# An encoder block on one core: the Fourier half scaled by ACT, its residual added later by an accumulating DMA, its wave tables made in two parts beforehand

## The chip, the core and the metric

The kernel runs on one NeuronCore of a Trainium2 chip. The core has engines that run side by side, each through its own instructions in order: TensorE (PE in the profile, with its weight loads as PEld), VectorE (DVE), ScalarE (ACT), GpSimd (POOL) and SyncE (SP), which here only issues DMAs. PE reads SBUF and writes PSUM. [...] POOL in this kernel works on SBUF alone and issues DMAs too. The metric is the time of the whole program on the device in microseconds, as the median of some runs. Before the change it is 2309.82 us (three runs, 2309.82 to 2311.7).

## What is computed

One layer of an encoder over 2048 tokens and 16 meta tokens (2064 in all), with 1024 channels, in float32. The input is normalized and projected once; a part of the projection goes to attention (4 query heads, 2 key and value heads of 128), a part, 4 groups of 128 channels, to a Fourier mix. Both halves are normalized by themselves, joined and projected back, and a residual is added; then comes an MLP of width 4096 with a squared relu, and a last normalization.

```python
f = jnp.fft.fft2(ug, axes=(1, 3), norm='ortho').real.astype(u.dtype)
y = jnp.einsum('blgc,gcd->blgd', f, w_f)
...
mixed = jnp.concatenate([rms_norm(attn, g_attn_out[i]), rms_norm(four, g_fourier_out[i])], axis=-1)
h = h + mixed @ w_out[i]
m = rms_norm(h, g_mlp[i])
h = h + jnp.square(jax.nn.relu(m @ w_up[i])) @ w_down[i]
...
return rms_norm(h, g_final)[:, N_META:]
```

The normalization of a half is one factor per token, so it can be applied after the product with `w_out`.

## The kernel before

**Products in parts.** A float32 operand of a large product is split in a high part (rounded by an ACT copy to `float32r`) and a low part (what is left, subtracted by DVE). `mm3` (L75 to L80) makes a product of three matmuls: high by high, high by low, low by high. The class `Split` makes the parts (L68 and L69; L71 and L72 with a factor). PE is thus fed by pairs of an ACT and a DVE instruction on nearly every operand.

**The stages in order.** First the input is normalized, transposed and projected (`prep`, `proj_u`, `proj_qkv`, `post`). The Fourier group's sequence is folded into even and odd parts in two large buffers, EV and UA. Then four transforms follow (`transform(0)` to `transform(3)`: cosine and sine, even and odd frequencies). Each makes partial sums `pa` over the channels, splits them into `ahi` and `alo`, and multiplies them with wave tables in `product`: 8 products `py` of 258 columns per transform, each summing over 2 (transforms 0 and 1) or 4 (2 and 3) full tables and one remainder table of 96 rows, which carries the high and low parts of a few rows in its own rows. `fourier` adds and subtracts the results back into EV and UA.

**Wave tables.** `load_tables` (from L484) loads a raw table of 128 rows and 516 columns by SP (L497), makes its high part by ACT (L503) and its low part by DVE (L506; L509 for 32 rows of the remainder table). There are 12 full and 4 remainder tables. Raw tables have 3 buffers, high parts 6, low parts 5. ACT's and DVE's table work of a transform is queued behind the last partial sums of the transform before (`last_acts`, `issue_after`).

**The Fourier half of the output projection.** `out_f` (L848 to L883) walks over 16 tiles of 128 tokens. For each it loads the tile of x into `xt` by SP (L859), splits the Fourier rows into `yh` and `yl`, and squares them by ACT (L869). POOL adds the four groups' squares in two steps, 256 and 128 columns wide (L872). PE sums them over the channels (L873), DVE and POOL make the factor `rf` from the sum (`rstd_of`, L188 and L190). Two halves of 512 columns are multiplied with `w_out` (`pof`), and DVE scales each by `rf` and adds x in one instruction (L881). The tile goes to `h_d` in DRAM by SP (L883).

**Attention beside it.** Attention runs in 16 units of 256 queries by 2 heads. Its scores, maxima, exponentials, sums and outputs `o` are interleaved with the transforms and with `out_f` by hand (`mix`, `att.upto`), and later with the MLP. The loads of queries, keys and values (q, kt, vt) are issued by POOL. Queries have one buffer, so a unit's queries are loaded when the scores of the unit before are done.

**The attention half.** `out_a(b)` (L937 on), for each of four blocks of 512 tokens, loads four tiles `h` from `h_d` by SP (L944), multiplies attention's output with `w_out` (`poa`), and DVE scales it by `ra` and adds it to `h` (L983). Then the MLP of the block follows (`transposes`, `up`, `down`, `final`).

**Order.** The program's text gives priorities; a planner assigns each engine's order, and that of the DMA queues, from its own estimates of when an operand is ready. So a load can stand earlier in a queue than in the text, but each queue is then run in that order: an instruction that waits holds up all that is behind it on its engine, DMA issues too.

Of the kernel before, what the change touches and what calls it, by code (L numbers as in the profile page):

```python
# [11 lines left out]
F32 = mybir.dt.float32  # L12
R32 = mybir.dt.float32r
AF = mybir.ActivationFunctionType
ALU = mybir.AluOpType
# [4 lines left out]
P = 128  # L20
# [14 lines left out]
REM = 96  # L35
MR = 96
CH = QUART // 2
CHP = 272
# [6 lines left out]
AHEAD = 30  # L45
FLEAD = 30
SKIP = 5
T_BUFS = (5, 6)
F_BUFS = (6, 7)
S_BUFS = 8  # L50
A_BUFS = 11
# [3 lines left out]
def f32v(ap):  # L55
    return ap.bitcast(F32)
# [26 lines left out]
def ins_of(x):  # L83
    return getattr(x, "ins", x)
# [49 lines left out]
def encoder_block(ctx: ExitStack, tc: tile.TileContext, x, meta, w_in, w_f,  # L134
                  w_out, w_up, w_down, g_fin, g_cols, g_rows, c_id, c_rope, c_dft, c_even, c_odd, c_rem, out):
    nc = tc.nc
    split = Split(nc)
    x = x[0]
    out = out[0]
# [58 lines left out]
    h_d = [dram.tile([P, D], F32, name=f"h_d{t}") for t in range(NT)]  # L198
# [273 lines left out]
        nc.vector.tensor_tensor(high, low, high, op=ALU.subtract)  # L472
        nc.scalar.copy(low, t)

    TW = 2 * CH
    last_acts = []
    ROWS = _rows()
    tables = {}

# [4 lines left out]
    def load_tables(tr):  # L484

        src, full, rest, n_tab = sources(tr)
        rem = ft.tile([P, NG, REM], F32, name=f"rem{tr}", tag="rem", bufs=1)
        nc.vector.memset(rem, 0.0)
        for o in (0, 32, 64):
            for lo, hi in rest:  # L490
                nc.vector.tensor_copy(rem[:, :, o:o + hi - lo], src[:, :, lo:hi])
                o += hi - lo
        tabs = []
        for nt in list(range(n_tab)) + [len(full)]:
            rows = P if nt < n_tab else REM
            raw = ft.tile([P, TW], F32, name=f"traw{tr}_{nt}", tag="traw", bufs=3)
            nc.sync.dma_start(raw[:rows], (c_even[tr, nt] if tr < 2 else c_odd[tr - 2, nt]) if rows == P else c_rem[tr])  # L497
            raw = raw.rearrange("p (c n) -> p c n", c=2)
            hi = ft.tile([P, 2, CHP], R32, name=f"thi{tr}_{nt}", tag="thi", bufs=T_BUFS[1])[:, :, :CH]
            with ExitStack() as behind:  # L500
                for i in last_acts:
                    behind.enter_context(tc.issue_after(i))
                nc.scalar.copy(hi[:rows], raw[:rows])  # L503
                if rows == P:
                    lo = ft.tile([P, 2, CHP], R32, name=f"tlo{tr}_{nt}", tag="tlo", bufs=T_BUFS[0])[:, :, :CH]
                    nc.vector.tensor_tensor(lo, raw, f32v(hi), op=ALU.subtract)  # L506
                    tabs.append((hi, lo))
                else:
                    nc.vector.tensor_tensor(hi[32:64], raw[32:64], f32v(hi[32:64]), op=ALU.subtract)  # L509
                    tabs.append(hi)  # L510
        tables[tr] = tabs, rem

    def transform(tr):

        src, full, rest, n_tab = sources(tr)
        if tr not in tables:
            load_tables(tr)
        tabs, rem = tables[tr]
        acts = []
        for nt in range(len(full) + 1):  # L520
            rows = P if nt < len(full) else REM
            ps = bank(f"pa{tr}_{nt}", (P, NG, P))
            for g in range(NG):
                a = src[:, g, full[nt]:full[nt] + P] if rows == P else rem[:, g, :]
                nc.tensor.matmul(ps[:rows, g, :], a, cw[tr % 2][:, g, :],
                                 start=True, stop=True)
            hi = fp.tile([P, NG, P], R32, name=f"ahi{tr}_{nt}", tag="ahi", bufs=F_BUFS[1])
            cp = nc.scalar.copy(hi[:rows], ps[:rows])
            if rows == P:
                lo = fp.tile([P, NG, P], R32, name=f"alo{tr}_{nt}", tag="alo", bufs=F_BUFS[0])  # L530
                nc.vector.tensor_tensor(lo, ps, f32v(hi), op=ALU.subtract)
                acts.append((hi, lo))
            else:
                sb = nc.vector.tensor_tensor(hi[64:96], ps[64:96], f32v(hi[64:96]), op=ALU.subtract)
                acts.append(hi)
                last_acts[:] = [ins_of(cp), ins_of(sb)]

        def product(g, c):
            ps = bank(f"py{tr}_{g}_{c}", (P, CH))
            for q in range(n_tab):  # L540
                hi, lo = acts[q + c * n_tab if tr < 2 else q]
                mm3(nc, ps, (hi[:, g, :], lo[:, g, :]), (tabs[q][0][:, c], tabs[q][1][:, c]), q == 0, False)
            nc.tensor.matmul(ps, acts[-1][:REM, g, :], tabs[-1][:REM, c], start=False, stop=True)
            return ps

        return product

    for j in range(LAST + 1):
# [16 lines left out]
        else:  # L565
            if j == 1:
                chan_dft()
            if j == LAST:
# [9 lines left out]
                ft = Lines(tc.alloc_tile_pool(name="ft", bufs=1, reuse_waits="tile"), small)  # L578
# [269 lines left out]
    def out_f():  # L848
        wt = {}
        for k in range(NG):  # L850
            for h in range(2):
                raw = wp.tile([P, 512], F32, name=f"wfr{k}_{h}", tag="wr", bufs=3)
                nc.sync.dma_start(raw, w_out[512 + k * P:512 + (k + 1) * P, h * 512:(h + 1) * 512])
                wt[k, h] = tuple(op_.tile([P, 512], R32, name=f"wf{e}{k}_{h}") for e in "hl")
                split(*wt[k, h], raw, c_fo(k))
            yield
        for t in range(NT):
            xt = op_.tile([P, D], F32, name=f"xo_{t}", tag="xo", bufs=2)
            nc.sync.dma_start(xt, x[t * P:(t + 1) * P, :])  # L859
            hi = op_.tile([P, NG, P], R32, name=f"yh_{t}", tag="yh", bufs=2)  # L860
            lo = op_.tile([P, NG, P], R32, name=f"yl_{t}", tag="yl", bufs=2)
            sq = op_.tile([P, NG, P], F32, name=f"ysq_{t}", tag="ysq", bufs=2)
            for par in range(2):
                for src, col, e, n in y_runs(par, 64 * t, 64 * t + 64):
                    y = src[:, :, col:col + n]
                    o = 2 * (e - 64 * t) + par
                    v = slice(o, o + 2 * n - 1, 2)
                    split(hi[:, :, v], lo[:, :, v], y)
                    nc.scalar.square(sq[:, :, v], y)  # L869
            ps = misc(f"pys_{t}", (P, 1))  # L870
            for n in (2, 1):
                nc.gpsimd.tensor_tensor(sq[:, :n], sq[:, :n], sq[:, n:2 * n], op=ALU.add)  # L872
            nc.tensor.matmul(ps, sq[:, 0], ones, start=True, stop=True)  # L873
            rf = rstd_of(op_, ps, 1, 512, "f")
            for h in range(2):
                ps = bank(f"pof_{t}_{h}")
                with tc.issue_after(ended[0]) if 2 * t + h >= 2 * NT - HELD else nullcontext():
                    for k in range(NG):
                        mm3(nc, ps, (hi[:, k, :], lo[:, k, :]), wt[k, h], k == 0, k == NG - 1)
                hs = slice(h * 512, (h + 1) * 512)  # L880
                nc.vector.scalar_tensor_tensor(xt[:, hs], ps, rf, xt[:, hs], op0=ALU.mult, op1=ALU.add)  # L881
                yield
            nc.sync.dma_start(h_d[t], xt)  # L883

# [52 lines left out]
    def out_a(b):  # L937

        b0, n = BLOCKS[b]
        T = 2 * n  # L940
        H[b] = hs = []
        for t in range(T):
            h = hps[b == 1].tile([P, D], F32, name=f"h_{b}_{t}", tag="h", bufs=4)
            nc.sync.dma_start(h, h_d[2 * b0 + t])  # L944
            hs.append(h)
        ps = misc(f"pas_{b}", (P, T))
        for t in range(T):
# [12 lines left out]
        for half in range(2):  # L960
            c = slice(half * 512, (half + 1) * 512)
# [29 lines left out]
        for t in range(T):  # L991
            nc.vector.scalar_tensor_tensor(part[t], sums[t][:, 1:2], 1.0 / D, part[t], op0=ALU.mult, op1=ALU.add)
            tag = "rs_m2" if b == 2 else "rs_m"
# [584 lines left out]
def _tables():  # L1578
# [13 lines left out]
    for tr in range(4):  # L1592
        starts, rest = _rows()[tr]
        token = _token(tr)
        if tr < 2:
            n_q = len(starts) // 2
            freq = [4 * np.arange(CH) + 2 + 2 * c for c in range(2)]
            full.append(np.stack([np.concatenate([_wave(tr, token(starts[c * n_q + q] + np.arange(P)), freq[c])
                                                  for c in range(2)], axis=1) for q in range(n_q)]))
        else:  # L1600
            freq = [2 * np.arange(c * CH, (c + 1) * CH) + 1 for c in range(2)]
            full.append(np.stack([_wave(tr, token(s0 + np.arange(P)), np.concatenate(freq)) for s0 in starts]))
        r = np.zeros((REM, 2 * CH), np.float32)
        for o in (0, 32, 64):
            for i, (lo, hi) in enumerate(rest):
                for c in ((i,) if tr < 2 else range(2)):
                    r[o:o + hi - lo, c * CH:(c + 1) * CH] = _wave(tr, token(np.arange(lo, hi)), freq[c])
                o += hi - lo
        rem.append(r)
    return np.eye(P, dtype=np.float32), rope, dft, np.stack(full[:2]), np.stack(full[2:]), np.stack(rem)  # L1610


_INS = ['x', 'meta_tokens', 'w_in', 'w_fourier', 'w_out', 'w_up', 'w_down', 'g_final']
# [27 lines left out]
```

## Time and profile before

| | |
|---|---|
| median of the runs | 2309.82 us |
| the profiled execution | 2310.59 us, of it 2308.8 us the span |
| PE busy | 2278.1 us (99% of the span) |
| weight loads busy | 1879.0 us (81%) |
| DVE busy | 1714.1 us (74%) |
| ACT busy | 1292.8 us (56%) |
| POOL busy | 204.6 us (9%) |
| moved by DMA | 307.23 MB |

The span runs from the first to the last instruction; the profiled execution's own time is a little longer. A row of a group of instructions has the line, engine and operation, out<-in by the program's names, the shapes and the count; after the bar the total busy time in us and the mean of one in ns; after the second bar the idle time of the engine just before them and what ended it. A row on one tile has the shortest, median and longest duration in ns and the first and last start in us. A row of waits reads: engine and line, what it waited for, the total in us, how often, the longest. PE's matmuls overlap, so that a busy PE can still lose time between two of them. DMA issues on POOL count as its instructions.

### The profile page before, as it was taken

Reading aid. Unit: us, or ns where it says so; the run is one execution under the profiler, and the core shown is the slowest. Engines: PE = TensorE matmul, PEld = TensorE weight load, DVE = VectorE, ACT = ScalarE, POOL = GpSimd, SP = SyncE. Lnnn points to the kernel's source line nnn. Section 1 sums busy time; section 2 is a strip of 40 time slices with the busy share of each in tenths; the row PEclk is TensorE's granted clock in tenths of the full one; section 3 lists DMA queues with packets and bytes.
Section 4 is the critical chain, followed back from the end, with each engine's and each line's share of the span. In section 5 each row is a group of like instructions: output and inputs, shape, how many; then the busy total and the mean of one; then the engine's idle time right before and its main releaser. Section 6 shows DMA issues by size and latency. Waiting matters only on the chain.

```text
span 2308.8 us, 29997 instructions
## 1 busy us (share of the span) xinstructions
PE 2278.1 (99%) x10822; PEld 1879.0 (81%) x10822; DVE 1714.1 (74%) x2431; ACT 1292.8 (56%) x2331; POOL 204.6 (9%) x244
## 2 busy tenths in 40 slices
PE   8999999999999999999999999999999999999998
PEld 7888987777788888888878888888888888888886
DVE  5435578999887876976886977886675656696786
ACT  6443355656675665665775675664555545543333
POOL 2212120233100000000000100000100000200000
PEclk9999999999999999999999999999999999999999
DMA  6343252543533322333242453325344444865442
GB/s 209 101 119 105 75 154 74 180 151 111 185 107 105 97 86 79 113 113 111 92 169 68 155 181 101 101 79 191 119 162 171 155 146 155 302 200 163 130 127 83
DMA packets 178069, 307.23 MB, mean 133 GB/s; under 512 B 14960, under 2 KB 63728, under 8 KB 177536
## 3 DMA queue, kind: packets, MB, share of 16 engines
q1 hardware_dynamic: 159280, 263.16, 34.7%
q0 software_dynamic: 18640, 42.16, 6.2%
q8 instruction: 85, 1.39, 0.2%
q14 instruction: 64, 0.52, 0.1%
HBM read 225.27 MB, written 79.99 MB: 132 GB/s over the span
## 4 chain that ended last, share of the span: by engine, by line
PE 70%; DVE 2%; DMA 1%; ACT 1%; issue 1%; POOL 0%; DVEq 0%; POOLq 0%; SPq 0%; ACTq 0%
PE pdn L78 5%; PE pdn L80 5%; PE pdn L79 5%; PE pup L80 5%; PE pup L78 5%; PE pup L79 5%; PE ux L78 2%; PE ux L79 2%; PE ux L80 2%; PE dx L78 2%; PE dx L79 2%; PE dx L80 2%; PE o L78 2%; PE o L79 2%; PE o L80 2%; PE s L78 2%
## 5 line engine op out<-in xcount | busy, mean ns | idle before, releaser
L78 PE MATMUL pup<-mT,wh_up 128*128 128x512 f32 x512 | 200.8, 393 | 0.7 <-ACT mT L71 0.7
L80 PE MATMUL pup<-mT,wl_up 128*128 128x512 f32 x512 | 200.9, 393 | 0.3 <-DVE wl_up L69 0.3
L79 PE MATMUL pup<-mT,wh_up 128*128 128x512 f32 x512 | 200.7, 392 | 0.0
L79 PE MATMUL pdn<-wl_dn,ah 128*128 128x512 f32 x512 | 200.6, 392 | 0.0
L78 PE MATMUL pdn<-wh_dn,ah 128*128 128x512 f32 x512 | 200.5, 393 | 0.0
L80 PE MATMUL pdn<-wh_dn,al 128*128 128x512 f32 x512 | 199.2, 391 | 0.0
L723 ACT COPY S<-s 128x512 f32<-128x512 f32 x256 | 148.8, 584 | 45.3 <-PE s L80 36.4
L68 ACT CAST wh_up<-wr_up 128x512 fp32r<-128x512 f32 x128 | 79.2, 621 | 158.7 <-PE pup L79 81.6
L782 DVE TENSOR_TENSOR S<-S,mb 128x1024 f32<-128x1024 f32 x128 | 156.5, 1232 | 10.0 <-ACT mb L753 10.0
L69 DVE TENSOR_TENSOR pl<-S,ph 128x512 fp32r<-128x512 f32 x196 | 132.8, 695 | 12.7 <-ACT ph L68 11.1
L68 ACT CAST ph<-S 128x512 fp32r<-128x512 f32 x196 | 119.9, 621 | 31.5 <-PE o L80 25.8
L69 DVE TENSOR_TENSOR wl_up<-wr_up,wh_up 128x512 fp32r<-128x512 f32 x128 | 87.2, 686 | 67.7 <-ACT wh_up L68 62.3
L783 ACT ACTIVATE S<-S 128x1024 f32<-128x1024 f32 x114 | 120.3, 1058 | 30.3 <-DVE S L782 30.0
L789 DVE TENSOR_TENSOR acc<-acc,S 128x1024 f32<-128x1024 f32 x110 | 134.2, 1220 | 0.8 <-ACT S L783 0.5
L68 ACT CAST wh_dn<-wr_dn 128x512 fp32r<-128x512 f32 x128 | 78.9, 619 | 98.3 <-PE pdn L80 47.2
L729 DVE TENSOR_TENSOR M<-M,S 128x1024 f32<-128x1024 f32 x96 | 118.5, 1234 | 15.1 <-ACT S L723 14.2
L68 ACT CAST ah<-a 128x1024 fp32r<-128x1024 f32 x56 | 58.5, 1049 | 120.9 <-issue 61.3
L69 DVE TENSOR_TENSOR wl_dn<-wr_dn,wh_dn 128x512 fp32r<-128x512 f32 x128 | 87.0, 686 | 51.4 <-ACT wh_dn L68 44.0
L78 PE MATMUL s<-q,kt 128*128 128x512 f32 (+1 forms) x272 | 113.2, 416 | 1.9 <-DMA q<-q_d 1.2
L78 PEld LDWEIGHTS pdn<-wh_dn,ah 128*128 128x128 f32 x512 | 96.1, 188 | 22.3 <-ACT r L1057 1.9
L78 PEld LDWEIGHTS pup<-mT,wh_up 128*128 128x128 f32 x512 | 96.2, 188 | 20.4 <-ACT mT L71 0.9
L80 PEld LDWEIGHTS pup<-mT,wl_up 128*128 128x128 f32 x512 | 96.2, 188 | 19.9 <-DVE wl_up L69 0.8
(326 smaller groups left out, 6427.6 us busy)
## 6 DMA issues: line engine op xcount, KB each, us to landing
wr_up<-in_w_up_dram SPq DMA_DIRECT2D x128, 256.0 KB, 2.8
wr_dn<-in_w_down_dram SPq DMA_DIRECT2D x128, 256.0 KB, 2.6
a<-s_d SPq DMA_DIRECT2D x42, 512.0 KB, 3.7
R<-in_w_up_dram SPq DMA_DIRECT2D x16, 1024.0 KB, 5.3
s_d<-s SPq DMA_DIRECT2D x64, 256.0 KB, 2.1
d<-in_w_down_dram SPq DMA_DIRECT2D x26, 512.0 KB, 5.0
s_d<-c SPq DMA_DIRECT2D x48, 256.0 KB, 2.0
x<-in_x_dram SPq DMA_DIRECT2D x16, 512.0 KB, 4.8
```

The source lines that it names most:

```text
L68: nc.scalar.copy(hi, src)
L69: self.low = nc.vector.tensor_tensor(lo, src, f32v(hi), op=ALU.subtract)
L78: nc.tensor.matmul(out, a[0], b[0], start=first, stop=False, skip_group_check=chain)
L79: nc.tensor.matmul(out, a[0], b[1], start=False, stop=False, skip_group_check=chain)
L80: nc.tensor.matmul(out, a[1], b[0], start=False, stop=last, skip_group_check=chain)
L723: nc.scalar.copy(S[:, i % 2], ps)
L729: nc.vector.tensor_tensor(M, M, S, op=ALU.max)
L782: nc.vector.tensor_tensor(S, S, mb, op=ALU.subtract)
L783: nc.scalar.activation(p, S, AF.Exp, scale=ISQ)
L789: nc.vector.tensor_tensor(acc, acc, p, op=ALU.add)
```

## The change

The wave tables come from the host in two parts: the high part rounded to 12 bits of mantissa, the low part what is left; the remainder table has its low rows in place. A table is one DRAM array of 128 rows by 2 parts by 576 columns (TROW), loaded by one DMA on POOL's queue, straight into the `float32r` tile. There are 6 buffers of 4608 bytes per partition (TABS) in place of three rings. The 16 ACT copies, the DVE subtractions and the `issue_after` of `load_tables` are gone.

In `out_f`, x isn't loaded. DVE instead of POOL adds the squares. ACT instead of DVE scales the product by `rf`, out of PSUM into `xt`, without x. In `out_a`, SP loads a tile of x into `h`, and POOL issues a DMA that adds the tile of `h_d` to it.

```diff
-T_BUFS = (5, 6)
+TABS = 6
+TROW = 576
...
-            rows = P if nt < n_tab else REM
-            raw = ft.tile([P, TW], F32, name=f"traw{tr}_{nt}", tag="traw", bufs=3)
-            nc.sync.dma_start(raw[:rows], (c_even[tr, nt] if tr < 2 else c_odd[tr - 2, nt]) if rows == P else c_rem[tr])
-            raw = raw.rearrange("p (c n) -> p c n", c=2)
-            hi = ft.tile([P, 2, CHP], R32, name=f"thi{tr}_{nt}", tag="thi", bufs=T_BUFS[1])[:, :, :CH]
-            with ExitStack() as behind:
-                for i in last_acts:
-                    behind.enter_context(tc.issue_after(i))
-                nc.scalar.copy(hi[:rows], raw[:rows])
-                if rows == P:
-                    lo = ft.tile([P, 2, CHP], R32, name=f"tlo{tr}_{nt}", tag="tlo", bufs=T_BUFS[0])[:, :, :CH]
-                    nc.vector.tensor_tensor(lo, raw, f32v(hi), op=ALU.subtract)
-                    tabs.append((hi, lo))
-                else:
-                    nc.vector.tensor_tensor(hi[32:64], raw[32:64], f32v(hi[32:64]), op=ALU.subtract)
-                    tabs.append(hi)
+            tab = ft.tile([P, 2, TROW], R32, name=f"tab{tr}_{nt}", tag="tab", bufs=TABS)
+            hi, lo = (tab[:, e, :2 * CHP].rearrange("p (c n) -> p c n", c=2)[:, :, :CH] for e in range(2))
+            if nt < n_tab:
+                nc.gpsimd.dma_start(tab, c_even[tr, nt] if tr < 2 else c_odd[tr - 2, nt])
+                tabs.append((hi, lo))
+            else:
+                nc.gpsimd.dma_start(tab[:REM, 0], c_rem[tr])
+                tabs.append(hi)
...
             xt = op_.tile([P, D], F32, name=f"xo_{t}", tag="xo", bufs=2)
-            nc.sync.dma_start(xt, x[t * P:(t + 1) * P, :])
...
-                nc.gpsimd.tensor_tensor(sq[:, :n], sq[:, :n], sq[:, n:2 * n], op=ALU.add)
+                nc.vector.tensor_tensor(sq[:, :n], sq[:, :n], sq[:, n:2 * n], op=ALU.add)
...
-                nc.vector.scalar_tensor_tensor(xt[:, hs], ps, rf, xt[:, hs], op0=ALU.mult, op1=ALU.add)
+                nc.scalar.activation(xt[:, hs], ps, AF.Copy, scale=rf)
...
-            nc.sync.dma_start(h, h_d[2 * b0 + t])
+            r0 = (2 * b0 + t) * P
+            nc.sync.dma_start(h, x[r0:r0 + P, :])
+            nc.gpsimd.dma_start(h, h_d[2 * b0 + t], accum_op=ALU.add)
...
+        hi, lo = _parts(r)
+        hi[32:64] = lo[32:64]
+        rem.append(_row(hi))
+    full = [np.stack([_row(v) for v in _parts(f)], axis=2) for f in full]
...
+def _parts(v):
+    m, e = np.frexp(v.astype(np.float64))
+    hi = np.ldexp(np.rint(m * 4096) / 4096, e).astype(np.float32)
+    return hi, v - hi
```

More of the change, by code (lines that the diff above doesn't have):

```diff
@@ L473, in fold_even @@
         nc.scalar.copy(low, t)
-    TW = 2 * CH
-    last_acts = []
     ROWS = _rows()
@@ L527, in transform @@
             hi = fp.tile([P, NG, P], R32, name=f"ahi{tr}_{nt}", tag="ahi", bufs=F_BUFS[1])
-            cp = nc.scalar.copy(hi[:rows], ps[:rows])
+            nc.scalar.copy(hi[:rows], ps[:rows])
             if rows == P:
@@ L533, in transform @@
             else:
-                sb = nc.vector.tensor_tensor(hi[64:96], ps[64:96], f32v(hi[64:96]), op=ALU.subtract)
+                nc.vector.tensor_tensor(hi[64:96], ps[64:96], f32v(hi[64:96]), op=ALU.subtract)
                 acts.append(hi)
-                last_acts[:] = [ins_of(cp), ins_of(sb)]
         def product(g, c):
@@ L1608, in _tables, with _row @@
                 o += hi - lo
-        rem.append(r)
+        hi, lo = _parts(r)
+        hi[32:64] = lo[32:64]
+        rem.append(_row(hi))
+    full = [np.stack([_row(v) for v in _parts(f)], axis=2) for f in full]
     return np.eye(P, dtype=np.float32), rope, dft, np.stack(full[:2]), np.stack(full[2:]), np.stack(rem)
+def _parts(v):
+    m, e = np.frexp(v.astype(np.float64))
+    hi = np.ldexp(np.rint(m * 4096) / 4096, e).astype(np.float32)
+    return hi, v - hi
+def _row(v):
+    out = np.zeros(v.shape[:-1] + (TROW,), np.float32)
+    for c in range(2):
+        out[..., c * CHP:c * CHP + CH] = v[..., c * CH:(c + 1) * CH]
+    return out
 _INS = ['x', 'meta_tokens', 'w_in', 'w_fourier', 'w_out', 'w_up', 'w_down', 'g_final']
```

## The prediction

> **What bounds the kernel now.** I read the busy table first, then the slices of time around the code that changes, then who waits for whom inside those slices. The busy table of the page:
>
> ```profile
> PE 2278.1 (99%) x10822; PEld 1879.0 (81%) x10822; DVE 1714.1 (74%) x2431; ACT 1292.8 (56%) x2331; POOL 204.6 (9%) x244
> ```
>
> PE is busy for 2278.1 of a span of 2308.8 us, so all the idle of the whole kernel is 30.7 us, and the change removes no matmul. It can gain only what PE stands idle (or waits unseen between overlapping matmuls) in the stages that it touches. The sums by stretch say where that is; the columns are PE, weight loads, DVE, ACT and POOL:
>
> ```profile
> 282.00:311.00 29.00, 29.00 (x132) 22.96 (x131) 23.06 (x51) 12.55 (x41) 4.28 (x4) 1.00 0.18 54
> 311.00:420.00 109.00, 107.00 (x663) 88.18 (x662) 92.70 (x148) 65.60 (x120) 13.80 (x20) 1.00 0.46 133
> 420.00:598.00 178.00, 172.10 (x768) 133.09 (x768) 167.18 (x238) 109.18 (x207) 57.85 (x56) 1.00 0.47 157
> ```
>
> 282 to 311 is where the first tables are made, 311 to 420 the four transforms, 420 to 598 the Fourier half of the output projection beside attention. PE idles for 0, 2.0 and 5.9 us there. In the third stretch DVE is busy for 167.18 of 178 us, nearly as full as PE, and ACT has 69 us free. The waits from 420 to 600 name the releaser (total us, times, longest):
>
> ```profile
> ACT yh L68 <- PE pof L79: 9.0, 7, 2.6
> PEld o L79 <- DVE pl L69: 6.8, 8, 2.0
> DVE xo L881 <- POOL rs_f L190: 3.9, 5, 1.7
> PE o L79 <- DVE pl L69: 3.9, 5, 1.6
> PEld pof L80 <- DVE yl L69: 3.0, 5, 0.9
> DVE xo L881 <- PE pof L80: 2.0, 2, 1.0
> PE pof L80 <- DVE yl L69: 1.1, 3, 0.5
> ```
>
> PE stands still for 3.9 + 1.1 = 5.0 us because a low part (pl, yl) comes late from DVE; counted at the weight loads, which stop earlier, it is 6.8 + 3.0 = 9.8 us. And DVE itself stands for 3.9 + 2.0 = 5.9 us in front of the scaling that is moved. So in this stage a shorter DVE queue is worth something; after 660 us it is not, since none of the changed work but sixteen loads lies there.
>
> **The Fourier half: scaling to ACT, squares to DVE.** The rows for what leaves DVE and what comes (groups of 420 to 598, then DVE's and ACT's nearest operations):
>
> ```profile
> L881 DVE SCALAR_TENSOR_TENSOR xo<-pof,rs_f,xo 128x512 f32<-128x512 f32 x32 | 23.7, 744 | 6.2 <-POOL rs_f L190 3.9 <-PE pof L80 2.0
> L823 DVE TENSOR_TENSOR sq<-sq,O 128x256 f32<-128x256 f32 x4 | 1.7, 415 | 0.0
> L188 DVE TENSOR_SCALAR ms_f<-pys 128x1 f32<-128x1 f32 x16 | 2.4, 148 | 0.1
> L723 ACT COPY S<-s 128x512 f32<-128x512 f32 x45 | 26.0, 582 | 9.7 <-PE s L80 7.1 <-DVE pl L69 2.3
> L1031 ACT ACTIVATE mt<-pmt,cols x8: 680/685/690, 1325.5 to 1337.8; 128x512 f32<-128x512 f32 x8
> L872 POOL TENSOR_TENSOR ysq<-ysq 128x256 f32<-128x256 f32 (+1 forms) x32 | 33.0, 1034 | 39.0 <-ACT ysq L869 37.8
> ```
>
> DVE loses 32 scalings, 23.7 us. It gains 16 adds of 256 columns at 0.415 and 16 of 128 columns, which lie between 0.148 (one column) and 0.415; I take the middle, 0.28, so 16 x 0.695 = 11.1 us. Net 12.6 us less.
>
> A second, smaller relief: DVE's instructions are slower here than elsewhere. In this stretch and over the whole span (the first two rows are of the stretch):
>
> ```profile
> L782 DVE TENSOR_TENSOR S<-S,mb 128x1024 f32<-128x1024 f32 x22 | 28.5, 1304 | 0.0
> L729 DVE TENSOR_TENSOR M<-M,S 128x1024 f32<-128x1024 f32 x18 | 23.3, 1293 | 0.5 <-ACT S L723 0.3
> L782 DVE TENSOR_TENSOR S<-S,mb 128x1024 f32<-128x1024 f32 x128 | 156.5, 1232 | 10.0 <-ACT mb L753 10.0
> L729 DVE TENSOR_TENSOR M<-M,S 128x1024 f32<-128x1024 f32 x96 | 118.5, 1234 | 15.1 <-ACT S L723 14.2
> ```
>
> That is 22 x 0.072 + 18 x 0.059 = 2.6 us in these two groups, in the stretch where POOL runs its 32 adds; I count 2 us of it as going with them; the bounds are 0, if something else slows them, and 2.6.
>
> ACT gains 32 scalings out of PSUM at 0.582 (plain copy) to 0.685 (scaled by a column), 18.6 to 21.9 us: 109.2 becomes at most 131 of 178. It takes over the wait for rs_f as well; behind it stand the score copies S and the casts ph and yh, which PE and DVE need. ACT waited 9.0 us for PE before yh alone, so I cost this at nothing in the middle case; if that cover is gone it is the 5.9 us that DVE waits today. DVE gets a new wait, for ACT's squares: POOL stood 37.8 us for them in 8 waits, but with nothing else in its queue; on DVE the subtractions pl and M stand behind. The bounds for this wait are 0 and the 5.9 us just freed.
>
> So DVE goes from 167.2 busy and 5.9 waiting to about 152.6 busy. What PE wins lies between 0 (the waits come back on ACT and DVE) and 9.8 us (all waits of the weight loads). I take 7.0: the 5.0 that PE is seen to stand, and two fifths of the 4.8 that only the weight loads show, since a load that waits often has a matmul still running over it.
>
> **The tables.** What goes (group rows of the raw table and its parts):
>
> ```profile
> L503 ACT CAST thi<-traw x16: 617/623/637, 282.8 to 395.1; 128x516 fp32r<-128x516 f32 x12, 96x516 fp32r<-96x516 f32 x4
> L506 DVE TENSOR_TENSOR tlo<-traw,thi x12: 632/690/698, 286.5 to 393.0; 128x516 fp32r<-128x516 f32 x12
> L509 DVE TENSOR_TENSOR thi<-traw,thi x4: 686/686/687, 296.8 to 397.0; 32x516 fp32r<-32x516 f32 x4
> PE s L78 <- DMA q<-q_d: 1.2, 1, 1.2
> PE pa L525 <- DVE alo L531: 0.5, 1, 0.5
> PE py L543 <- DVE ahi L534: 0.2, 1, 0.2
> ```
>
> ACT is rid of 16 x 0.623 = 10.0 us, DVE of 12 x 0.690 + 4 x 0.686 = 11.0 us. Of the 2.0 us that PE idles between 311 and 420, the last three rows give 1.2 to a load of q, which this doesn't touch, and 0.7 to DVE. I take a gain of 0.5; bounds 0 and 2.0.
>
> What comes: 16 loads on POOL's queue, 12 of 576 KB and 4 of 216 KB, into six slots. The first two transforms fill all six early. The third needs five: three slots are free when the first is done, two when the second is done, and its own partial sums and scores of attention still lie ahead of its products, so I cost these at nothing. The fourth is tight. One slot is free since the second; the other four come free as the third transform's last product passes. Before, the raw data already stood in SBUF and only 0.6 us of ACT and 0.7 us of DVE lay between. PE's order there, and what such loads take to land:
>
> ```profile
> 391.20 0.28 PE L80 MATMUL py<-thi,alo 128*128 128x258 f32 x1
> ...
> 392.03 0.28 PE L543 MATMUL py<-thi,ahi 96*128 96x258 f32 x1
> ...
> 398.44 0.39 PE L78 MATMUL py<-thi,ahi 128*128 128x258 f32 x1
> ...
> 400.36 0.39 PE L543 MATMUL py<-thi,ahi 96*128 96x258 f32 x1 [0.20 <-DVE ahi L534]
> kt<-k_d POOLq DMA_DIRECT2D x5, 608.0 KB, 5.4
> hs<-h_d POOLq DMA_DIRECT2D x4, 512.0 KB, 9.9
> q<-q_d POOLq DMA_DIRECT2D x16, 512.0 KB, 4.9
> 1181.69 0.74 POOL L697 DMA_DIRECT2D q<-q_d  x1 [6.23 <-PE s L80]
> ```
>
> Four issues of 0.74 from 391 on put the last at about 393.3. A single 608 KB load lands in 5.4 us, one of four sent together in 9.9: the last table is there at 398.7 to 403.2. The first product's last matmul ran at 400.36, so PE waits for 0 to 2.9 us. I take 1.0, as attention's matmuls, planned between the products, can stand in front. [...]
>
> **The residual.** The 16 loads of x move from SP in the projection to SP in the attention half, and 16 accumulating DMAs of 512 KB take the place of SP's loads of h_d, on POOL's queue, each behind its x:
>
> ```profile
> L944 SPq DMA_DIRECT2D h<-h_d x16: 320/424/738, 449.3 to 1343.3; - x16
> L983 DVE SCALAR_TENSOR_TENSOR h<-poa,rs_a,h x32: 735/744/752, 604.6 to 1640.2; 128x512 f32<-128x512 f32 x32
> h<-h_d SPq DMA_DIRECT2D x16, 512.0 KB, 5.4
> 1177.36 0.41 SPq L944 DMA_DIRECT2D h<-h_d  x1
> 1187.45 0.43 SPq L944 DMA_DIRECT2D h<-h_d  x1
> ```
>
> The first h is loaded 604.6 - 449.3 = 155 us before its use, the last 1640.2 - 1343.3 = 297 us before the last use, so an accumulation (no row shows one) hides even at twice the 9.9 us that is the longest landing here. What doesn't is POOL's queue: an accumulation that waits for x holds up what is queued behind it, the load of q that the next scores need, rs_a, rs_m, keys and values. Bounds below at the rival; I take 0.3.
>
> **Sum.** -7.0 - 0.5 + 1.0 + 0.3 = -6.2 us on the profiled execution's own 2310.59 (span 2308.8 and 1.8 around it): 2304.4. That execution is 0.8 above the median of the runs, 2309.82, so the time is 2303.6, 0.27% faster.
>
> **Rivals.** (a) The waits only move. ACT waits for rs_f and DVE for the squares, and PE finds pl as late as before. For it: ACT, too, runs in order, and rs_f still comes from POOL. Against it: DVE is relieved of 12.6 + 2 us in a stretch where it had 10.8 us left. PE keeps 1 us of gain and loses 1 at the tables: 2309.8. (b) The last tables come late and cost the full 2.9, and the gain in the projection is only the 5.0 seen, less half of 5.9 in new waits: 2.9 - 2.0 = +0.9, so 2310.7, no change. (c) Slower: POOL's queue. At 1177.36 to 1187.45 the third block's h are loaded, and q at 1181.69 stands between. If x lands 5.4 us after its issue and all four accumulations stand ahead of q, q goes out at 1187.45 + 5.4 + 0.7 = 1193.6, 11.9 us late, and PE, in order, stands at the next scores: +11.9 - 6.2 = +5.7, so 2315.5. One ahead costs 1182.8 + 0.7 - 1181.7 = 1.8. At 6.2 us, the third one, the gain is gone. Against it: the planner orders by its own due times, and x is due after q there.
>
> **Chances.** Forecast 0.55; all bounds good (9.8 and 2.0 gained, no costs: -11.8, so 2298.0) 0.07; (a) 0.15; (b) 0.08; (c) 0.15. Two measurements of this kernel differ by some 0.1%, so 0.2%, 4.6 us, is about what can be told from no change. Faster, below 2305.2, is 0.40 of the forecast's 0.55, since its terms alone scatter by some 4 us, and the good case: 0.47. Within 0.2% are the rest of the forecast, (a) and (b): 0.38. Slower is (c): 0.15. The range goes from 2298.0, the good bounds, to 2313.0, half the way from no change to (c); the forecast's own is 2299 to 2308.
>
> **What would show it.** Right: between 420 and 598 DVE's busy time falls by 12 to 16 us, the waits of PE and weight loads for pl and yl fall below 4 us, the DVE rows S and M go back towards 1.23, and the fourth transform's first product starts within 3 us of its partial sums. Wrong: PE waiting on ACT's S or ph, DVE waiting on ysq, PE waiting on a table or on q behind an accumulation. If the gap between 420 and 598 closes and the total doesn't fall, something after 600 took it.

## The result: 0.4% slower, outside the range

| | before | after |
|---|---|---|
| median of the runs | 2309.82 us | 2318.69 us |
| lowest to highest | 2309.26 to 2311.7 us | 2317.9 to 2321.86 us |
| ratio, 95% interval | | 1.0038 [1.0029, 1.0048] |
| span of the profiled execution | 2308.8 us | 2317.0 us |
| PE busy | 2278.1 us | 2280.1 us |
| DVE busy | 1714.1 us | 1684.1 us |
| moved by DMA | 307.23 MB | 311.23 MB |

The forecast was 2303.6, with a range up to 2313.0. DVE has 30 us less to do, as the change meant, and the kernel is 8.9 us slower. All views and times inside a kernel below are of one profiled execution each. Below, the changed kernel's names with its own line numbers: scaling L870, sums of squares L861, load of x into h L934, accumulating load L935, table loads L497 and L500.

Where the time went can be read from one row. `pas` is the small product that opens the attention half of each of the four blocks, so its first start marks the end of the Fourier stages, and its last start the opening of the last block. Before, then after (the last field before the forms is first and last start in us):

```profile
L948 PE MATMUL pas<-ones,sq x32: 164/250/250, 595.9 to 1617.3; 128*128 128x1 f32 x32
```

```profile
L939 PE MATMUL pas<-ones,sq x32: 164/250/250, 594.6 to 1626.2; 128*128 128x1 f32 x32
```

Up to the first `pas` the changed kernel is 1.3 us ahead. From the first to the last it takes 1031.6 us in place of 1021.4. So up to there, where the forecast had its gain, little came, and something later took 10.2 us.

**After 600 us.** The waits of PE from 1170 to 1400 in the changed kernel (total us, times, longest); the kernel before has there a single wait of 0.3:

```profile
PE pm_m L727 <- DVE M L708: 3.0, 1, 3.0
PE o L79 <- ACT ph L69: 2.7, 1, 2.7
```

Both lie where h of a block is loaded while the block before still runs its MLP. The sums by stretch (columns as in the prediction, the last three being PE's clock, the share of the DMA engines and GB/s), before and after:

```profile
1180.00:1190.00 10.00, 9.94 (x49) 7.47 (x47) 6.80 (x10) 4.61 (x8) 0.74 (x1) 1.00 0.93 305
1190.00:1200.00 10.00, 9.91 (x46) 8.07 (x46) 9.96 (x15) 9.97 (x19) 0.00 (x0) 1.00 0.50 179
1343.00:1353.00 10.00, 10.00 (x52) 8.11 (x51) 5.82 (x8) 3.01 (x7) 1.43 (x2) 1.00 0.92 298
1353.00:1363.00 10.00, 10.00 (x47) 7.81 (x46) 10.00 (x15) 9.91 (x17) 0.00 (x0) 1.00 0.34 111
```

```profile
1180.00:1190.00 10.00, 10.00 (x52) 7.92 (x51) 6.41 (x9) 4.08 (x6) 2.54 (x3) 1.00 0.94 264
1190.00:1200.00 10.00, 7.35 (x25) 5.59 (x25) 8.43 (x12) 9.00 (x16) 1.72 (x2) 0.83 1.04 285
1343.00:1353.00 10.00, 9.28 (x41) 7.21 (x39) 5.50 (x7) 3.48 (x7) 3.98 (x5) 1.00 0.98 252
1353.00:1363.00 10.00, 7.49 (x32) 5.83 (x33) 5.33 (x7) 4.11 (x7) 0.76 (x1) 0.83 1.09 315
```

Before, the DMA engines were full for 10 us at each reload and then at half or a third. Now they are full for 20, and move less per full slice (264 GB/s at 0.94, 305 at 0.93 before). In the second slice PE runs 25 and 32 matmuls in place of 46 and 47: part of the time it stands, and for part of it its clock is down (0.83 as the mean of the slice). What is late is the weights of the MLP. The longest wait of ACT from 1340 to 1365, and then the landing of the up and of the down projection's weights over the whole kernel, before and after:

```profile
ACT wh_up L69 <- DMA wr_up<-in_w_up_dram: 6.5, 1, 6.5
```

```profile
DMA to landing us min/median/max: 2.6/2.8/4.5
DMA to landing us min/median/max: 2.4/2.6/5.7
```

```profile
DMA to landing us min/median/max: 2.6/2.8/8.4
DMA to landing us min/median/max: 2.4/2.6/13.0
```

ACT runs in order. While it waits 6.5 us for a weight, the scores' copies behind it wait too, DVE's maximum M waits for them, and PE waits for M (the 3.0 above). Near 1190 it waits 3.0 us for a weight of the down projection, the cast ph stands behind it, and PE waits for ph (the 2.7).

**The transforms.** Between 311 and 420 PE is busy for 105.0 us in place of 107.0:

```profile
311.00:420.00 109.00, 104.99 (x642) 86.04 (x640) 81.79 (x131) 57.85 (x104) 19.09 (x30) 0.98 0.50 146
420.00:598.00 178.00, 173.91 (x791) 137.27 (x790) 154.86 (x244) 130.83 (x244) 27.03 (x28) 1.00 0.42 132
```

POOL's order there, and the wait that PE has:

```profile
323.82 0.64 POOL L497 DMA_DIRECT2D tab<-c_odd  x1 [10.00 <-PE py L81]
324.47 0.72 POOL L687 DMA_DIRECT2D q<-q_d  x1
325.17 1.46 POOL L654 DMA_DIRECT2D kt<-k_d  x2
```

```profile
PE s L79 <- DMA kt<-k_d: 2.3, 1, 2.3
```

The first table of the third transform waits 10.0 us on POOL for its slot, and attention's first queries and keys stand behind it. The first scores start at 333.0 in place of 329.8.

**The projection stage.** In the second row above DVE has 12.3 us less than before, ACT 21.7 more, PE 1.8 more. DVE's rows there:

```profile
L772 DVE TENSOR_TENSOR S<-S,mb 128x1024 f32<-128x1024 f32 x26 | 31.4, 1217 | 0.0
L719 DVE TENSOR_TENSOR M<-M,S 128x1024 f32<-128x1024 f32 x18 | 22.0, 1221 | 1.5 <-ACT S L713 1.1
L861 DVE TENSOR_TENSOR ysq<-ysq 128x256 f32<-128x256 f32 (+1 forms) x32 | 11.1, 354 | 0.2
```

The first accumulating load stands here too, just ahead of a load of q on POOL's queue (450.76 and 451.51). PE's wait for that q, and what the load of q took to land:

```profile
PE s L79 <- DMA q<-q_d: 1.7, 1, 1.7
```

```profile
DMA to landing us min/median/max: 8.4/8.4/8.4
```

In the kernel before, the load of q near this place landed in 5.2 us, and PE didn't wait for it.

### The profile page after: what moved, and what is told of

The parts are those of the page before. It is cut to its first block, busy times and chain, and to the rows that moved or that the text cites. A ratio compares the mean times of both kernels' runs of the same rounds, so it can differ in the third digit from the quotient of the medians.

```text
span 2317.0 us, 29998 instructions
## 1 busy us (share of the span) xinstructions
PE 2280.1 (98%) x10822; PEld 1882.1 (81%) x10822; DVE 1684.1 (73%) x2415; ACT 1302.2 (56%) x2347; POOL 192.4 (8%) x244
## 2 busy tenths in 40 slices
DMA packets 178068, 311.23 MB, mean 134 GB/s; under 512 B 14960, under 2 KB 63728, under 8 KB 177536
## 4 chain that ended last, share of the span: by engine, by line
PE 77%; DVE 3%; DMA 3%; ACT 2%; issue 1%; POOL 1%; POOLq 0%; DVEq 0%; ACTq 0%; SPq 0%
PE pdn L79 5%; PE pdn L81 5%; PE pdn L80 5%; PE pup L80 4%; PE pup L79 4%; PE pup L81 4%; PE ux L79 2%; PE ux L81 2%; PE ux L80 2%; PE dx L80 2%; PE dx L79 2%; PE dx L81 2%; PE s L79 2%; PE s L81 2%; PE s L80 2%; PE o L79 2%
```

## The experiments

First theory, from the traces alone: x and h_d together are twice the bytes of the reload, they collide with the weights, and that costs some 10 us; the table at the head of POOL's queue costs some 3; scaling and squares gain between 4 and 5. All times of whole kernels below are medians, with the ratio to the kernel before in the same runs; "against before" is the difference to its median in the same runs, since the runs were made on several chips. The changed kernel has +8.9 in this measure.

### Each part undone

**e1**: only the residual as before.

```diff
-                nc.scalar.activation(xt[:, hs], ps, AF.Copy, scale=rf)
+                nc.vector.scalar_tensor_tensor(xt[:, hs], ps, rf, xt[:, hs], ...)   # x loaded into xt ahead
-            nc.sync.dma_start(h, x[r0:r0 + P, :])
-            nc.gpsimd.dma_start(h, h_d[2 * b0 + t], accum_op=ALU.add)
+            nc.sync.dma_start(h, h_d[2 * b0 + t])
```

> The residual goes back to where it was (x loaded ahead of the projection, VectorE multiplies and adds it, h read back by SP alone); tables and squares stay as in the changed kernel (2318.69). Theory, the doubled reload of h: the two reloads near 1180 and 1345 lose their 10.5 us of excess and the projection stage (420 to 598) gives back its gain of 4.7 and up to 2 more, because VectorE now has the residual and the squares: 2313 to 2315, and the weight loads of the up projection land within 5 us again. Rival, the tables or the squares cost it: the time stays above 2317.

Measured: 2308.23, 0.9992 [0.9983, 1.0001], against before -1.9. The 10 us are the residual's, as the theory has it. But the projection gave nothing back, so that the time is 4.8 below the theory's range: the first `pas` starts at 592.5, earlier than with the residual moved (594.6). That step of the theory fell.

**e2**: only the tables as before. `load_tables` and the host's arrays are those of the kernel before.

> The wave tables go back to what they were (one part loaded by SP, split by ScalarE and VectorE); residual and squares stay as in the changed kernel (2318.69). Theory: q and the keys are issued at once on POOL's queue, TensorE's 2.3 us wait on the keys near 331 goes, and the stage 300 to 420 gives back its 3.1 us: 2315 to 2316. Rival, the table load at the head of POOL's queue is hidden and the 3.1 us is the lower clock of that stage: 2318 to 2319.

Measured: 2322.67, 1.0055 [1.0042, 1.0067], against before +12.5. Worse, where 3 us less was expected: both expectations missed. The keys are early again (first scores at 330.2), but between 420 and 595 PE waits for ACT's ph (2.4), q and the squares (1.6 each) and M (1.2), and the first `pas` comes at 598.1. Why is not shown: ACT makes the tables' parts again, but the last of them starts at 396.1.

### What in the reload costs

**e4** (plain load in place of the accumulating one) and **e5** (that, and no load of x):

```diff
-            nc.sync.dma_start(h, x[r0:r0 + P, :])                                    # e5 only
-            nc.gpsimd.dma_start(h, h_d[2 * b0 + t], accum_op=ALU.add)
+            nc.gpsimd.dma_start(h, h_d[2 * b0 + t])
```

> The accumulating load of h is a plain load on POOL's queue that overwrites x: same bytes from DRAM, same queue, same order, no read and add at the destination (it leaves the residual x out of the result). Theory, bytes and their collision with the weight stream: 2317.5 to 2319.5. Rival, the accumulation itself is what is slow: at least 5 us less, 2308 to 2313, with the landings of the up weights back at 5 us.

> SP's load of x into h is left out and h comes by one plain load on POOL's queue (it leaves the residual x out of the result): half the bytes, POOL's queue keeps its sixteen loads. Theory, the doubled bytes: 8 to 11 us less, 2308 to 2311, and no idle of over 2 us on TensorE at 1180 to 1200 and 1343 to 1363. Rival, POOL's queue (q and the keys behind h): no change, 2317.5 to 2319.5.

Measured: e4 2311.84, 1.0007 [0.9998, 1.0016], against before +1.7; e5 2310.84, 1.0003 [0.9994, 1.0012], +0.7. So the bytes alone are not it: with the same bytes, and no addition at the destination, most of the loss is gone. The theory fell here, and the rival (the accumulation itself) was near. Both leave x out of the result. They were measured apart from the changed kernel, so their sizes were taken again below.

### Squares, tables and the order on POOL's queue

**e6** is the changed kernel, **e7** is e1, both with the table loads of the third and fourth transform behind the first keys:

```diff
+            with tc.issue_after(kv0[0]) if kv0 else nullcontext():   # kv0: the last load of the first keys
                 nc.gpsimd.dma_start(tab, ...)
```

**e8** is e1 with the squares summed by POOL again (only the tables changed); **e9** is the kernel before with L872 on `nc.vector` (only the squares).

> The changed kernel (2318.69), with the table loads of the third and fourth transform put on POOL's queue behind the first keys instead of ahead of q. Theory, that order makes the first scores late: the first scores start about 3 us earlier (at 330 instead of 333) and the time falls by 1 to 2.5 us, to 2316 to 2317.7. Rival, the wait is made up for later in the stage, or the tables are now late for the third transform: no change or slower, 2318 to 2321.

> The kernel with the residual where it was (2308.23), and the same order of the table loads: theory 2306 to 2307.3; rival, no change, 2307.8 to 2310.

> Of the change only the tables: residual as before, squares summed by GpSimd as before. The two together, without the residual, gave 2308.23 against 2310.16. Theory, the squares give that: GpSimd's sums are what made VectorE's rows of S and M 1.30 instead of 1.22 us, so tables alone are within 1 us of the kernel before (2309.5 to 2311) and the S and M rows stay near 1.3. Rival, the tables give it (they took 4.0 us off the kernel with the residual moved): 2306.5 to 2308.5.

> Of the change only the squares' sums on VectorE, all else as before. Theory, they give the gain: 2307.5 to 2309, rows of S and M near 1.22 in the projection stage in place of 1.30, VectorE's busy time there about the same as before (11.1 us of sums added, as much saved on the longer rows). Rival, VectorE has 11 us more to do in the stage that it bounds: 2311 to 2315.

| | median | ratio | against before |
|---|---|---|---|
| e6 all parts, keys first | 2315.18 | 1.0027 [1.0017, 1.0037] | +5.1 |
| e7 squares and tables, keys first | 2305.78 | 0.9981 [0.9972, 0.9990] | -4.3 |
| e8 tables alone | 2314.52 | 1.0019 [1.0011, 1.0028] | +4.4 |
| e9 squares alone | 2308.57 | 0.9993 [0.9984, 1.0001] | -1.5 |

*The order.* e6 is 3.8 better than the changed kernel by this measure, e7 2.4 better than e1: the first scores start at 330.0 and 329.0, the wait for the keys is gone, and the stretch's clock is 1.00 again; both come out up to 1 us below their theory. Tables alone with the keys late (e8) lose 4.4, more than either theory allowed; e9's gain is the one expected. e8 and e1 differ in the place of the sums alone: beside the tables, moving them to DVE is worth 6.4 by this measure (on two chips), 4.8 of it between the first scores and the first `pas`.

*Moving the residual brings the projection nothing in sum.* e6 and e7 differ in the residual alone. Sums from 420 to 595, e6 and then e7:

```profile
420.00:595.00 175.00, 171.58 (x774) 134.88 (x773) 152.34 (x242) 128.94 (x242) 27.67 (x29) 1.00 0.44 136
```

```profile
420.00:595.00 175.00, 172.16 (x769) 134.20 (x769) 167.09 (x269) 109.01 (x205) 24.25 (x24) 1.00 0.50 165
```

DVE has 14.8 us more in e7 and is as full as in the kernel before, and PE is no later: the first `pas` starts at 590.0 (590.7 in e6). e7 as a whole is 9.4 us faster than e6 in the same runs. The nothing in the projection is a sum of two things, though. PE's second wait for q, the one behind the first accumulating load, is in the four traces that have this load ahead of it (1.7 us in the changed kernel, 1.1 in e6, 1.6 in e2, 2.0 in e11), where q landed in 7.7 to 8.6 us. With a plain load ahead of it in the same order (e4, e5, and e14 below) PE doesn't wait for it, and it landed in 5.5 to 5.7. The first `pas` of e14 is at 588.6, 1.4 us earlier than e7's: so a gain of about that size from the scaling's move was there, as far as single executions can tell, and the accumulation took it back.

*The squares shorten the other DVE rows.* Rows of DVE in the same stretch, tables alone (e8, sums on POOL) and squares alone (e9, sums on DVE):

```profile
L779 DVE TENSOR_TENSOR acc<-acc,S 128x1024 f32<-128x1024 f32 x19 | 24.7, 1301 | 0.0
L871 DVE SCALAR_TENSOR_TENSOR xo<-pof,rs_f,xo 128x512 f32<-128x512 f32 x31 | 23.1, 746 | 7.5 <-POOL rs_f L191 5.3 <-PE pof L81 2.0
L70 DVE TENSOR_TENSOR pl<-S,ph 128x512 fp32r<-128x512 f32 x30 | 21.6, 753 | 0.2 <-ACT ph L69 0.2
```

```profile
L789 DVE TENSOR_TENSOR acc<-acc,S 128x1024 f32<-128x1024 f32 x20 | 24.4, 1218 | 0.0
L881 DVE SCALAR_TENSOR_TENSOR xo<-pof,rs_f,xo 128x512 f32<-128x512 f32 x32 | 23.9, 747 | 4.9 <-POOL rs_f L190 4.4
L69 DVE TENSOR_TENSOR pl<-S,ph 128x512 fp32r<-128x512 f32 x32 | 21.2, 684 | 1.3 <-DMA o_d<-ol 1.3
```

acc goes from 1301 to 1218, pl from 753 to 684, and xo stays. PE's wait for pl, 3.9 us before, is 0.8 in e9, although DVE is busy for as long as before (166.0 against 164.2 us from 420 to 595). Two further rows of e8 speak less clearly: S took 1226 ns and M 1245, where the expectation had both near 1.30. Taking each instruction by itself settles it. In the kernel before, from 420 to 598, the 25 pl that ran with none of POOL's sums beside them took 682 ns in the mean, the 7 with one beside them 907; S took 1211 (16 of them) and 1552 (6), xo 744 (29) and 747 (3). In e8 only one of 23 S had a sum beside it. The shortest, median and longest pl, before and in e9:

```profile
L69 DVE TENSOR_TENSOR pl<-S,ph x32: 673/682/1223, 465.3 to 597.7; 128x512 fp32r<-128x512 f32 x32
```

```profile
L69 DVE TENSOR_TENSOR pl<-S,ph x32: 680/684/693, 464.7 to 593.6; 128x512 fp32r<-128x512 f32 x32
```

In the kernel before, acc took 1213 ns with no sum beside it (16 of them) and 1344 with one (3). So S, acc and pl, which read two tiles in SBUF, were longer beside a sum, and xo, which reads one from PSUM, wasn't.

### Where and how the reload collides

**e10** adds x in the projection stage, **e11** uses the accumulating load for tiles 0 to 7 only; both from e6:

```diff
+            nc.gpsimd.dma_start(xt, x[t * P:(t + 1) * P, :], accum_op=ALU.add)       # e10, ahead of the store to h_d
-            nc.sync.dma_start(h, x[r0:r0 + P, :])                                     # e10; e11 for b > 1
-            nc.gpsimd.dma_start(h, h_d[2 * b0 + t], accum_op=ALU.add)                 # the same
+            nc.sync.dma_start(h, h_d[2 * b0 + t])                                     # the same
```

**e12** is e1 with a load of x on SP's queue ahead of each load of h, which overwrites it; **e13** is e1 with h read back on POOL's queue.

> Residual by ScalarE's scaling and an accumulating transfer, but the transfer adds x to the tile of the projection stage, before it is stored; h is read back by SP alone; tables behind the keys. The same kernel with VectorE's residual gave 2305.78. Theory, an accumulating load costs where it meets the weight stream of the up projection, and the projection stage has room: 2304.5 to 2307. Rival, sixteen accumulating loads cost wherever they are (behind q and the values on POOL's queue, or by their engine time): 2309 to 2313.

> Residual by accumulating load only for the first two blocks of rows (tiles 0 to 7), VectorE's for tiles 8 to 15, whose h is read back by SP alone; tables behind the keys. With VectorE's residual for all: 2305.78, with the accumulating load for all: 2315.18. Theory, only the reloads of the last two blocks (near 1180 and 1345) meet the weight stream: 2305 to 2307. Rival, each of the sixteen costs the same: half the difference, 2310 to 2311.

> The kernel with the residual where it was (2308.23), with one more load on SP's queue ahead of each reload of h: x into the same tile, which the load of h then overwrites. It adds the changed kernel's bytes alone, without POOL's queue and without accumulation. From the two plain-load kernels (2311.84 with x, 2310.84 without) the bytes are worth 1.0: 2308.7 to 2310. Rival, the bytes in the weights' own queue are what made them late: 2312 to 2316.

> The kernel with the residual where it was (2308.23), with h read back on POOL's queue instead of SP's, one plain load each: POOL's queue alone, without x and without accumulation. The kernel without x load and without residual gave 2310.84, and it differs from this one only by ScalarE's scaling in place of VectorE's multiply and add, which the front of the kernel did not show: 2310 to 2311.5. Rival, POOL's queue is free and those 2.6 us were the scaling on ScalarE: 2307.5 to 2309.

| | median | ratio | against before |
|---|---|---|---|
| e10 | 2315.8 | 1.0017 [1.0008, 1.0027] | +6.0 |
| e11 | 2303.86 | 0.9977 [0.9969, 0.9986] | -5.9 |
| e12 | 2317.81 | 1.0036 [1.0023, 1.0049] | +8.0 |
| e13 | 2315.48 | 1.0027 [1.0017, 1.0037] | +5.7 |

e11 came out 1.1 below its theory's range: the eight accumulating loads of the first two blocks cost nothing that the total shows. From the first to the last `pas` it takes 1022.6 us, just as e7 (in an execution that took 2308.22 in all). e11 and e7 beat both kernels.

e10 fell in two groups: nine executions at 2314.7 to 2317.0, three at 2306.1 to 2308.7. The profiled one is among the nine and shows a stall; there is no trace of the three without the loss, so that this stall is the whole difference is not shown. Sums by stretch, and DVE's wait from 580 to 605:

```profile
590.00:600.00 10.00, 5.26 (x19) 3.60 (x17) 4.70 (x5) 6.56 (x10) 0.86 (x1) 0.81 0.95 264
600.00:610.00 10.00, 10.00 (x33) 8.13 (x33) 6.87 (x10) 1.95 (x4) 1.94 (x1) 0.67 0.34 99
```

```profile
DVE pl L70 <- DMA o_d<-ol: 5.7, 1, 5.7
```

The store of attention's output holds the buffer that the next pl needs. It is late while the engines are full (0.95) with accumulating loads in what they move; PE stands 3.3 us at the longest, and the clock is down in two slices (0.81 and 0.67). So neither theory's place was right: by e11 it isn't each load that costs, and here it isn't the weights that suffer.

e12 and e13 missed: I had expected 1 and 2.6 us more than e1, and got 10.0 and 7.6 (the difference to e1's -1.9). In both, too, PE's idle leads to `ACT ph <- DMA o_d<-oh` (2.5 us in e12 near 1205, 3.5 in e13 near 465). In e12 PE waited 2.2 us for the late keys besides, and 1.9 for tables. By the first `pas` (597.4 and 599.0, e1's 592.5) 4.9 us of e12's loss and 6.5 of e13's lie ahead of 600; from the first to the last, e12 takes 6.1 us more than e1, and e13 2.2.

### The division, taken again with the keys first

**e14** is e6 with the plain load of e4. **e15** is e7 with the extra load of e12. **e16** is the complement of e11: accumulating loads for tiles 8 to 15.

> The changed kernel with the tables behind the keys (2315.18), its accumulating loads of h made plain loads on POOL's queue that overwrite x (it leaves the residual x out of the result). Without the doubled reload the same kernel took 2305.78, so 9.4 us are to be divided. Theory, from the stretch after 595 us in the traces (1713 us with one load on SP, 1719 with x and a plain load, 1722.5 with x and an accumulating one): 6 for the second load, 3.5 for the accumulation, so 2311 to 2312.5. Rival 1, the accumulation is all of it: 2305.5 to 2307. Rival 2, the accumulation is none of it: 2314.5 to 2316.

> The kernel with VectorE's residual and the tables behind the keys (2305.78), with x loaded ahead of each reload of h into the same tile on SP's queue and overwritten. Theory, the second 512 KB of each tile costs 6 wherever it is issued: 2311 to 2312.5. Rival, the bytes are free and the 9.6 us of the same edit with the tables ahead of the keys was the late keys alone: 2305.5 to 2308.

> The complement of the kernel with accumulating loads for the first two blocks (2303.86): accumulating loads for tiles 8 to 15 alone, VectorE's residual for tiles 0 to 7. Theory, the two reloads near 1180 and 1345 carry the whole cost of about 9.4: 2313.5 to 2316. Rival, the cost needs all sixteen: 2308 to 2311.

| | median | ratio | against before |
|---|---|---|---|
| e14 | 2309.26 | 0.9998 [0.9989, 1.0007] | -1.2 |
| e15 | 2313.12 | 1.0015 [1.0006, 1.0024] | +2.7 |
| e16 | 2316.53 | 1.0031 [1.0019, 1.0044] | +6.1 |

From e7 (-4.3) over e14 (-1.2, on another chip) to e6 (+5.1): the second load costs 3.1, the accumulation 6.3. By first and last `pas` (1022.6, 1027.3 and 1031.7 us) it is 4.7 and 4.4; so both cost, and the division is known to about 2 us. The 2 us fit the first `pas`, which is 2.1 earlier in e14 than in e6: that part of the accumulation's cost lies ahead of 600, where q comes late. e14 came out 1.7 us below what was expected, e15 and e16 0.6 and 0.5 above it. e16 has the whole cost of e6, and a little more, with half of the loads: the last two blocks carry it. e15 is dearer than e14 with the same bytes at the reload. On SP's queue the load of h waits for x to land, and stores and weights stand behind it; SP's waits from 1160 to 1380, and ACT's from 1185 to 1215:

```profile
SPq L940 <- DMA h<-in_x_dram: 15.4, 7, 5.4
```

```profile
ACT ph L69 <- DMA o_d<-oh: 2.6, 1, 2.6
```

What the accumulation does to the engines is in the time that the packets of POOL's queue took (packets, MB, share of 16 engines' span), in e7, e14 and e6:

```profile
q0 software_dynamic: 20816, 50.13, 7.2%
```

```profile
q0 software_dynamic: 23120, 58.51, 8.2%
```

```profile
q0 software_dynamic: 23120, 58.51, 9.2%
```

Sixteen plain loads add 1.0% of the span, sixteen accumulating ones of the same bytes 2.0%. Over 2310 us that is 1.4 us of all 16 engines per 512 KB, and 2.9. These are times of packets, which overlap in full slices (a share of 1.09 above), so the engines may need less. As an estimate from them: four tiles took 5.8 us as plain loads; if x costs as much, and the accumulation another 11.6, that is 17.3 us at a reload in whose slice the engines were at 0.93 already.

## Why the prediction was wrong

1. **"so an accumulation (no row shows one) hides even at twice the 9.9 us"**. This step failed, and with it the forecast. The h did come in time: PE waits for no h in the changed kernel. I asked whether the moved transfers are late for their own reader, and not what they make late: by the estimate above three times the DMA time of the old reload, at 1180 and 1345, beside weights that ACT, in order, must have. Cost: 9.4 us (e6 against e7), on a term that I had put at 0.3; e11 and e16 put it at the last two blocks. The row to ask was the stretch's DMA share, 0.93 and 0.92 before the change.

2. **Rival (c)** had the place (1177 to 1187), the sign and a time 3.2 below the measured one (2315.5), but not the mechanism there: q went out at 1180.36, before the accumulations, and PE waits for no q after 1170. So its nearness is in the main luck. The mechanism was at work once, at the first block: with one accumulating load ahead of q PE waited 1.7 us, where (c) had 1.8 for one ahead, and chiefly because q itself took 8.4 us to land. I gave it 0.15.

3. **"What PE wins ... I take 7.0."** From the first scores to the first `pas` the kernel takes 261.6 us in place of 266.1: 4.5 gained, within the bounds. But the term was put together from the wrong part. I took it that a shorter DVE queue brings pl earlier; e6 against e7 shows 23.7 us of scaling on or off DVE worth under 1 us there in sum, e14 against e7 about 1.4 without the late q. With the sums off POOL, which had stretched DVE's rows (my "second, smaller relief"), PE's wait for pl went from 3.9 to 0.8 in e9, with DVE just as busy. How much of the old wait the stretched rows are is not shown: of the four DVE instructions ahead of the longest one, 1.6 us, a single acc was stretched, by 0.2. By medians the squares alone are worth 1.5, and their interval touches no change; beside the tables (e8 against e1) they are worth 6.4.

4. **The sizes of the instructions** were right: 32 sums took 11.1 us (11.1 predicted), the scaling 685 ns, the upper of the two rows given, DVE 154.9 busy (152.6). S and M fell to 1217 and 1221. Rival (a), waits that only move, was partly there: PE waits 2.1 us for ACT's ph in this stage, and pl's waits are gone.

5. **"So I cost these at nothing"** for the third transform's tables failed, **"I take 1.0"** for the fourth's was too much. No wait of PE for a table shows at the fourth. At the third the tables were not late; the load that waited for its slot made q and the keys late behind it. I had counted three free slots once the first transform is done, and so it was, but POOL stood 10.0 us in front of the load until its last product. With the clock that came down (0.98 from 311 to 420) the first scores were 3.2 us later than before; by e6 it is 3.8 us. The 16 table loads took POOL 0.52 to 0.75 us each to issue and landed in 5.7 us (median), where a load of 608 KB took 5.4 before.

6. **The tables' gain of 0.5** was too small once the keys go first: e7 against e9, 2.8 us in the same runs, the tables and the order together. That e2 lost, and e8 too, shows that these parts don't add up: what a part is worth depends on the others. Why the tables alone lose is shown only in part: the keys come late in e8 (first scores at 332.6) as in e1, which gained.

What stays open: e12 and e13 against e4 and e5, where the same kind of edit cost 1 to 3 us on one chip and 7.6 to 10.0 on another. In e13's trace PE's matmuls from 465 to 475 lose 4.9 us of the 7.6 against the usual times from one start to the next, after stores that landed in 6.4 and 6.5 us (2.8 and 4.2 in e1), with a DMA share of 0.90 and 0.85 in their last 4 us. It may be the same collision at another place. Whether POOL's queue by itself costs anything, I can't tell.

## What to carry over

A transfer that has hundreds of microseconds of slack for its own reader can still cost time, by what it delays while the DMA engines are full (here 9.4 us, e6 against e7, with shares of 1.02 to 1.05 in e6's slices): look at the DMA share of the slice where it will run, and at which short transfers (weights, stores that free a buffer) an in-order engine waits for there (ACT 6.5 us for one weight). An accumulating load is no free addition; here its packets took twice the time of a plain load's of the same bytes (2.0% against 1.0% of the span), and only in the first two blocks did it cost nothing in the total (e11). A nearly full engine need not be the bound: look at how long others wait for it (in e7 DVE was busy for 167 of 175 us, and PE waited 2.7 us for it). An engine that runs beside another can stretch its instructions (pl here, 682 ns in the median and 1223 at the longest, with POOL's sums beside it), so look at their longest beside their median. And a DMA that must wait for its slot belongs behind the loads that need not wait (POOL stood 10.0 us in front of one here, and the first scores came 3.2 us later than before).

## What the runs showed of the hardware

- **A lower clock came behind some short stalls.** After PE stood 2.7 and 3.0 us, the granted clock of the slice was 0.83, in the same slices before, with no stall, 1.00. From 1196.16 to 1199.54 the matmuls of the changed kernel start 427 ns apart in place of 227, so nearly half as fast for 3.4 us. The length of the stall alone doesn't decide it: one of 1.6 us (e8, at the keys) came with 0.89 over 15 us, and those of 2.4 and 2.2 us in e15 with 1.00 in their slices.
- **Full engines moved unequal amounts.** From 1180 to 1190 e14 moved 349 GB/s at a share of 0.96, the changed kernel, with accumulation, 264 at 0.94 (its rows are above; these are e14's):

```profile
1180.00:1190.00 10.00, 8.79 (x41) 6.63 (x39) 8.55 (x12) 7.58 (x12) 1.60 (x3) 1.00 0.96 349
1343.00:1353.00 10.00, 8.41 (x44) 6.68 (x43) 5.36 (x7) 4.29 (x7) 1.99 (x3) 1.00 1.09 387
```

- **Issuing an accumulating load** took POOL 888 ns (median of the changed kernel), a plain one of the same size 560 (e14); landing took 7.0 us in e6 and 5.1 in e14 (medians).
- **DVE's pl, S and acc beside one of POOL's sums** took longer in the kernel before (means of 907 against 682 ns, 1552 against 1211, 1344 against 1213; the longest pl 1223, 1.8 times the usual). xo, with an input in PSUM, did not (747 against 744).
